# Six transposes of a hybrid decoder layer moved from TensorE to VectorE, and the convolution's step rate set from 0.6 to 0.5

## The chip, the cores and the metric

The kernel runs on one core of one Trainium2 chip. The metric is the device time of one execution in microseconds (us), the median of several runs. The engines named below are TensorE (PE in the profile, PEld its weight loads), VectorE (DVE), ScalarE (ACT), GpSimd (POOL) and SyncE (SP, which issues the DMAs).

## The reference, cut to what matters

One layer, 256 tokens, model width 2048, float32. One projection gives the inputs of three branches, and each branch has its own output projection:

```python
h = rmsnorm(x, g_mix[l])
proj = h @ w_in[l]
u_glu, q_da, k_da, v_da, q_xa, gate_pre = jnp.split(proj, split_idx, axis=-1)

# conformer branch: GLU, causal depthwise convolution of 31 taps, layer norm over channels, swish
a, b = jnp.split(u_glu, 2, axis=-1)
u = a * jax.nn.sigmoid(b)
u = lax.conv_general_dilated(u, w_dw..., padding=[(CONV_WIDTH - 1, 0)],
                             feature_group_count=CONV_CH) + b_dw
y_conv = jax.nn.silu(layernorm(u, g_ln, b_ln)) @ w_conv_out[l]

# differential attention: rotary q and k, two softmaxes per head
q = apply_rope(q_da.reshape(bsz, seq, DA_HEADS, 2, DA_HEAD_DIM), cos, sin)
k = apply_rope(k_da.reshape(bsz, seq, DA_HEADS, 2, DA_HEAD_DIM), cos, sin)
y_da = diff_attention(q, k, v, lam, lambda_init, g_subln[l], w_da_out[l])
y_xa = memory_cross_attention(q_xa, mem_n, w_mem_kv[l], w_xa_out[l])

merged = gates[:, :, 0] * y_conv + gates[:, :, 1] * y_da + gates[:, :, 2] * y_xa
x = x + merged @ w_mix_out[l]
x = x + jnp.square(jax.nn.relu(rmsnorm(x, g_mlp[l]) @ w_up[l])) @ w_down[l]
return rmsnorm(x, g_final)
```

## The kernel before

**Weight groups.** All weights are streamed in order, in groups of 512 output columns (`group`). A group accumulates two PSUM tiles (`acc0` and `acc1`, one for each 128 tokens) over its k-tiles of 128 rows. Weights come in *pairs* of two k-tiles: SyncE loads `raw` (128x1024), ScalarE rounds it to `whi` (L325), VectorE computes `wlo`, the rest (L326, called a weight split here). TensorE then does three products per k-tile and token tile (L346 to L348), 12 matmuls per pair. `raw`, `whi` and `wlo` have four buffers each, so VectorE can be at most four pairs ahead of TensorE. A group with 2048 rows has 8 pairs, one with 1024 rows has 4.

**Order of the groups.** Four groups for the GLU, four for the memory's keys and values, two for the cross-attention's q (xq), two for q, two for k, two for v. Then, for each of four column chunks, three gate groups and the branch outputs in the order cross-attention (reads `xaT`), differential attention (reads `daT`), convolution (reads `cvT`). Then the mixing projection and the MLP.

**Side work.** What must happen between the groups is written as generators ("tasks") in lanes. After each pair `side_step` gives every lane's first task a tick. A task does one step for each unit of credit, and its rate is the credit per tick. When a group needs an input, it calls `finish` on the task that makes it, and the task's remaining steps are then written down at once. A scheduler at build time orders the instructions of each engine from priorities and an estimate of times; on the chip each engine's queue runs in that order.

**The work around the change.**
- `evac_rope` (L731 on) rotates q or k on VectorE when a group ends, into `rot`. The task `transpose_plain` (L261) then transposes it: eight 128x128 transposes on TensorE into the PSUM tile `tr`, copied by ScalarE (L269) into `qT` or `kT`. There are four such groups.
- `conv_half` (L509) does the same for half of the convolution's channels (`sig` into `uT`), then 31 steps of four tap instructions on VectorE (L518, L522). Both halves are in the lane `conv`, one behind the other, at the rate `CONV_RATE`. With the four steps of the transposes each half has 35 steps.
- `conv_norm` (L528) follows in that lane with some 31 steps at rate 1: sums over channels (L536), mean by a matmul into `pm` (L538), subtraction (L541), squares on ScalarE (L546), their sum (L550), a matmul into `pvar` (L554), square root on ScalarE (L557), reciprocal and a correction (L559 to L564), multiplication (L567), then for each of eight channel blocks sigmoid and affine on ScalarE (L573, L575), a product (L577) and the two parts of `cvT` (L578, L579). The first convolution output group reads `cvT`.
- `block_transpose2` (L235) exists already: 16 `STREAM_TRANSPOSE` instructions on VectorE, each moving 32x32 blocks of a 32x256 slice, in four steps of four. Each is ordered behind the weight split that was written last. It serves the memory keys (`kxT`), the cross-attention's q (`xqT`) and later inputs.
- `products` (L879 on) evacuates the three branch outputs on VectorE: `mg` from the cross-attention (L886), then `gate` and `mg` for the other two (L888, L892).

Of the kernel before, what the change touches and what calls it, by code (L numbers as in the profile page):

```python
# [10 lines left out]
F32 = mybir.dt.float32  # L11
# [8 lines left out]
P = 128  # L20
D = 2048
S = 256
NT = S // P
# [4 lines left out]
EPS = 1e-6  # L28
G = 512
KB = 2  # L30
CONV_RATE = 0.6
NORM_RATE = 1.0
WARM = 10
WB = 4
# [73 lines left out]
def decoder_layer_kernel(  # L108
# [6 lines left out]
    nc = tc.nc  # L115
# [6 lines left out]
    psum = ctx.enter_context(tc.tile_pool(name="psum", bufs=2, space=PSUM))  # L122
# [5 lines left out]
    def spawn(gen, lane="t", rate=1.0, hold=0):  # L128
        t = Task(gen, rate, hold)
        lanes[lane].append(t)  # L130
        return t
# [11 lines left out]
    def later(ins, first):  # L143

        tc.add_manual_dep(
            ins.ins, first.ins.name,
            mybir.DependencyInfo(mybir.DependencyClass.NoSync, mybir.DependencyReason.DATA),
            reason="issue order",
        )

    def finish(*tasks):
        for t in tasks:
            if t is not None:
                t.finish()
# [16 lines left out]
    def transpose(dst, src):  # L171
        k = src.shape[0]
        nc.tensor.transpose(dst, src, ident[:k, :k])  # L173
# [10 lines left out]
    def vcol(nm, i):  # L184
        return vec[:, col[nm] + i : col[nm] + i + 1]
# [10 lines left out]
    def both(f):  # L196
        seen = []

        def g(t, ps):
            seen.append(ps)  # L200
            if len(seen) == NT:
                f(seen)

        return g

    def by_tok(a):
        return [a[:, t, :] for t in range(NT)]

    chain = []

    def link(hi, lo):
# [6 lines left out]
    def scaled_parts(st, i, dst, kt, n, gname):  # L218

        his = [  # L220
            nc.scalar.activation(  # L221
                dst.hi(kt + c), st[:, i + c : i + c + 1, :], AF.Copy, scale=vcol(gname, kt + c)
            )
            for c in range(n)
        ]
        los = [
            nc.vector.scalar_tensor_tensor(
                dst.lo(kt + c), st[:, i + c : i + c + 1, :], vcol(gname, kt + c),
                dst.hi(kt + c).bitcast(F32), ALU.mult, ALU.subtract,
            )  # L230
            for c in range(n)
        ]
        return his[-1], los[-1]

    def block_transpose2(src, dst):  # L235

        B = 32
        out_v = dst.rearrange("p j (t s) -> p t j s", t=NT)
        in_v = src.rearrange("p t (j c k) -> p t j c k", c=P // B, k=B)
        for q in range(P // B):  # L240
            for c in range(P // B):
                ins = nc.vector.transpose(  # L242
                    out_v[c * B : (c + 1) * B, :, :, q * B : (q + 1) * B], in_v[q * B : (q + 1) * B, :, :, c, :]
                )
                later(ins, lo_mark[0])
            yield

    def to_parts_dve(src, dst, kt0, gname=None):

        st = work.tile([P, G // P, S], F32, tag="chunk", name="st", bufs=4)  # L250
        yield from block_transpose2(src, st)
        for b in range(0, G // P, 2):
            k = kt0 + b
            if gname is None:
                nc.scalar.copy(dst.hi(k, 2), st[:, b : b + 2, :])  # L255
                nc.vector.tensor_tensor(dst.lo(k, 2), st[:, b : b + 2, :], dst.hi(k, 2).bitcast(F32), op=ALU.subtract)
            else:
                scaled_parts(st, b, dst, k, 2, gname)
            yield

    def transpose_plain(src, dst, kt0, nkt):  # L261

        for b in range(0, nkt, 2):
            ps = psum.tile([P, 2, S], F32, tag="tr", name="tr")
            for c in range(2):
                for t in range(NT):
                    transpose(ps[:, c, t * P : (t + 1) * P], src[t][:, (b + c) * P : (b + c + 1) * P])
            yield
            nc.scalar.copy(dst[:, kt0 + b : kt0 + b + 2, :], ps)  # L269
            yield  # L270


# [219 lines left out]
    uT = units.tile([P, 8, S], F32, tag="unit", name="uT")  # L492
# [15 lines left out]

    def conv_half(g):  # L509
        u = sig[g]  # L510
        yield from transpose_plain(by_tok(u), uT, g * 4, 4)
        cbs = range(g * 4, g * 4 + 4)
        for d in range(TAPS):
            for cb in cbs:
                i = (TAPS - 1 - d) * 8 + cb
                w = taps[:, i : i + 1]
                if d == 0:
                    ins = nc.vector.tensor_scalar(  # L518
                        conv[:, cb, :], uT[:, cb, :], w, vcol("b_dw", cb), ALU.mult, ALU.add
                    )  # L520
                else:
                    ins = nc.vector.scalar_tensor_tensor(  # L522
                        conv[:, cb, d:], uT[:, cb, : S - d], w, conv[:, cb, d:], ALU.mult, ALU.add
                    )
                later(ins, mark[0])
            yield
# [55 lines left out]
    def evac_a(g):  # L582
        def f(ps):
            for t in range(NT):
                nc.vector.scalar_tensor_tensor(
                    sig[g][:, t, :], ps[t], rinv["x"][:, t : t + 1], sig[g][:, t, :], ALU.mult, ALU.mult
                )
            conv_tasks.append(spawn(conv_half(g), "conv", CONV_RATE))
        return both(f)
# [139 lines left out]
    qk_tasks = []  # L729

    def evac_rope(dst, g):  # L731
        def f(ps):
            finish(t_tables)
            H2 = DH // 2
            rot = work.tile([P, NT, G], F32, tag="chunk", bufs=4, name="rot")
            for t in range(NT):
                sc = rinv["x"][:, t : t + 1]
                cs = cosT[:, t, :].unsqueeze(1).to_broadcast([P, 8, H2])
                sn = sinT[:, t, :].unsqueeze(1).to_broadcast([P, 8, H2])
                pv8 = ps[t].rearrange("p (a d) -> p a d", d=H2)  # L740
                ac = work.tile([P, 8, H2], F32, tag="t2k", name="ropec", bufs=4)
                as_ = work.tile([P, 8, H2], F32, tag="t2k", name="ropes", bufs=4)
                nc.vector.scalar_tensor_tensor(ac, pv8, sc, cs, ALU.mult, ALU.mult)
                nc.vector.scalar_tensor_tensor(as_, pv8, sc, sn, ALU.mult, ALU.mult)
                c2 = ac.rearrange("p (m h) d -> p m h d", h=2)
                s2 = as_.rearrange("p (m h) d -> p m h d", h=2)
                o2 = rot[:, t, :].rearrange("p (m h d) -> p m h d", h=2, d=H2)
                nc.vector.tensor_tensor(o2[:, :, 0, :], c2[:, :, 0, :], s2[:, :, 1, :], op=ALU.subtract)
                nc.vector.tensor_tensor(o2[:, :, 1, :], c2[:, :, 1, :], s2[:, :, 0, :], op=ALU.add)
            qk_tasks.append(spawn(transpose_plain(by_tok(rot), dst, g * 4, 4)))  # L750
        return both(f)

    def evac_v(g):
# [276 lines left out]
```

## Time and profile before

| what | value |
|---|---|
| median of three runs | 1585.04 us (1584.47 to 1587.35) |
| profiled execution, its own time | 1584.57 us |
| its span, first to last instruction | 1582.0 us |
| PE busy | 1567.4 us, 99% of the span |
| DVE busy | 1130.4 us, 71% |
| ACT busy | 782.9 us, 49% |
| granted TensorE clock, mean | 0.998 of full speed |

A busy time is the sum of an engine's intervals. A step on one engine is best read from the starts of consecutive instructions, since neighbours overlap a little. The difference between the execution's own time and its span is 2.57 us, outside the instructions.

### The profile page before, as it was taken

What the parts mean: (1) busy time and instruction counts of PE and PEld (TensorE: products, weight loads), DVE (VectorE), ACT (ScalarE), POOL (GpSimd) and SP (SyncE); (2) the same over time, 40 slices, a digit from 0 to 9 for tenths busy, and PEclk for the clock granted to TensorE, in tenths of its full rate; (3) what the DMA queues carried; (4) which work ended last, traced back from release to release, by engine and by line L of the source; (5) the groups of instructions that cost most, each with busy time, mean ns of one, the idle gap of its engine ahead of it and who ended that gap; (6) DMA issues with size and microseconds to landing.
All of it is one profiled execution on the core that took longest, in us unless ns stands there. A gap on an engine that the chain in (4) does not pass through costs nothing.

```text
span 1582.0 us, 18995 instructions
## 1 busy us (share of the span) xinstructions
PE 1567.4 (99%) x6956; PEld 1296.6 (82%) x6956; DVE 1130.4 (71%) x1639; ACT 782.9 (49%) x1007; POOL 23.3 (1%) x35
## 2 busy tenths in 40 slices
PE   9999999999999999999999999999999999999997
PEld 7888788888888888888888788888888888888886
DVE  5699998887877456474598798447864687548864
ACT  7655445454784444444444555335534454445543
POOL 1000000010000000000000000000000000000000
PEclk9999999999999999999999999999999999999999
DMA  9776575556556666667766666666666666666663
GB/s 345 238 247 193 154 219 162 154 151 200 152 172 195 198 192 196 192 192 207 260 188 199 186 195 188 197 194 190 195 195 192 187 196 197 192 197 187 194 195 129
DMA packets 158732, 308.93 MB, mean 195 GB/s; under 512 B 9792, under 2 KB 10048, under 8 KB 158512
## 3 DMA queue, kind: packets, MB, share of 16 engines
q1 hardware_dynamic: 157104, 303.60, 63.0%
q0 software_dynamic: 960, 3.57, 0.8%
q8 instruction: 54, 0.88, 0.2%
q10 hardware_dynamic: 576, 0.56, 0.1%
q14 instruction: 38, 0.31, 0.1%
HBM read 305.60 MB, written 2.10 MB: 194 GB/s over the span
## 4 chain that ended last, share of the span: by engine, by line
PE 95%; DVE 3%; issue 1%; ACT 0%; DMA 0%; POOLq 0%; POOL 0%; ACTq 0%; DVEq 0%
PE acc L346 31%; PE acc L347 31%; PE acc L348 31%; DVE wlo L326 1%; DVE kxT L242 1%; DVE conv L522 1%; PE xs L678 0%; PE xo L711 0%; DVE st L242 0%; PE ds L773 0%; PE do L824 0%; PE tr L173 0%; DMA xt<-in_x_t_dram 0%; ACT whi L325 0%; PE xpt L173 0%
## 5 line engine op out<-in xcount | busy, mean ns | idle before, releaser
L326 DVE TENSOR_TENSOR wlo<-raw,whi 128x1024 fp32r<-128x1024 f32 (+1 forms) x561 | 684.4, 1221 | 413.0 <-ACT whi L325 409.0
L325 ACT CAST whi<-raw 128x1024 fp32r<-128x1024 f32 (+1 forms) x561 | 589.8, 1052 | 689.5 <-PE acc L348 641.7
L347 PE MATMUL acc<-wlo,xT_hi 128*128 128x512 f32 x768 | 300.2, 392 | 1.0 <-DVE wlo L326 1.0
L346 PE MATMUL acc<-whi,xT_hi 128*128 128x512 f32 x768 | 298.3, 395 | 2.8 <-ACT whi L325 2.8
L348 PE MATMUL acc<-whi,xT_lo 128*128 128x512 f32 x768 | 298.7, 392 | 0.0
L346 PE MATMUL acc<-whi,x1T_hi 128*128 128x512 f32 x512 | 198.2, 389 | 1.1 <-ACT x1T_hi L221 1.1
L347 PE MATMUL acc<-wlo,x1T_hi 128*128 128x512 f32 x512 | 199.0, 389 | 0.0
L346 PE MATMUL acc<-whi,ff_hi 128*128 128x512 f32 x512 | 198.7, 390 | 0.0
L347 PE MATMUL acc<-wlo,ff_hi 128*128 128x512 f32 x512 | 198.6, 389 | 0.0
L348 PE MATMUL acc<-whi,x1T_lo 128*128 128x512 f32 x512 | 198.4, 389 | 0.0
L348 PE MATMUL acc<-whi,ff_lo 128*128 128x512 f32 x512 | 197.9, 389 | 0.0
L346 PEld LDWEIGHTS acc<-whi,xT_hi 128*128 128x128 f32 x768 | 144.7, 189 | 32.7 <-ACT whi L325 3.0
L347 PEld LDWEIGHTS acc<-wlo,xT_hi 128*128 128x128 f32 x768 | 144.5, 188 | 31.3 <-DVE wlo L326 2.1
L348 PEld LDWEIGHTS acc<-whi,xT_lo 128*128 128x128 f32 x768 | 144.5, 188 | 29.9
L242 DVE STREAM_TRANSPOSE st<-ru 32x256 f32<-32x256 f32 x256 | 111.6, 436 | 4.1
L346 PEld LDWEIGHTS acc<-whi,x1T_hi 128*128 128x128 f32 x512 | 96.1, 188 | 21.5 <-ACT x1T_hi L221 1.6
L346 PEld LDWEIGHTS acc<-whi,ff_hi 128*128 128x128 f32 x512 | 96.1, 188 | 21.1 <-ACT ff_hi L255 1.4
L347 PEld LDWEIGHTS acc<-wlo,x1T_hi 128*128 128x128 f32 x512 | 96.1, 188 | 20.1 <-DVE wlo L326 0.2
L348 PEld LDWEIGHTS acc<-whi,ff_lo 128*128 128x128 f32 x512 | 96.1, 188 | 20.0
L347 PEld LDWEIGHTS acc<-wlo,ff_hi 128*128 128x128 f32 x512 | 96.1, 188 | 19.9
L348 PEld LDWEIGHTS acc<-whi,x1T_lo 128*128 128x128 f32 x512 | 96.1, 188 | 19.9
L522 DVE SCALAR_TENSOR_TENSOR conv<-uT,taps,conv 128x255 f32<-128x255 f32 (+29 forms) x240 | 98.2, 461 | 0.3
(197 smaller groups left out, 1376.0 us busy)
## 6 DMA issues: line engine op xcount, KB each, us to landing
raw<-in_w_in_dram SPq DMA_DIRECT2D x191, 512.0 KB, 4.3
raw<-in_w_up_dram SPq DMA_DIRECT2D x128, 512.0 KB, 3.8
raw<-in_w_down_dram SPq DMA_DIRECT2D x128, 512.0 KB, 4.7
raw<-in_w_mem_kv_dram SPq DMA_DIRECT2D x32, 512.0 KB, 4.6
raw<-in_w_mix_out_dram SPq DMA_DIRECT2D x32, 512.0 KB, 4.7
raw<-in_w_xa_out_dram SPq DMA_DIRECT2D x16, 512.0 KB, 4.8
raw<-in_w_da_out_dram SPq DMA_DIRECT2D x16, 512.0 KB, 4.7
raw<-in_w_conv_out_dram SPq DMA_DIRECT2D x16, 512.0 KB, 4.7
```

Source lines behind the costliest of these rows:

```text
L242: ins = nc.vector.transpose(out_v[c * B : (c + 1) * B, :, :, q * B : (q + 1) * B], in_v[q * B : (q + 1) * B, :, :, c, :])
L325: hi = nc.scalar.copy(whi[:, cs, :], raw[:, cs, :])
L326: lo_mark[0] = nc.vector.tensor_tensor(wlo[:, cs, :], raw[:, cs, :], whi[:, cs, :].bitcast(F32), op=ALU.subtract)
L346: nc.tensor.matmul(ps[t], hi[:, tt], whi[:, c, :], start=kt == 0, stop=False)
L347: nc.tensor.matmul(ps[t], hi[:, tt], wlo[:, c, :], start=False, stop=False)
L348: return nc.tensor.matmul(ps[t], lo[:, tt], whi[:, c, :], start=False, stop=kt == nkt - 1)
L522: ins = nc.vector.scalar_tensor_tensor(conv[:, cb, d:], uT[:, cb, : S - d], w, conv[:, cb, d:], ALU.mult, ALU.add)
```

## The change

`transpose_plain` and its helper are removed. The six places that used it, q and k (two groups each) and the convolution's input (two halves), call `block_transpose2`. `CONV_RATE` goes from 0.6 to 0.5, one convolution step for every two pairs. Line numbers of the later code fall by 14.

```diff
-CONV_RATE = 0.6
+CONV_RATE = 0.5
...
-    def by_tok(a):
-        return [a[:, t, :] for t in range(NT)]
...
-    def transpose_plain(src, dst, kt0, nkt):
-
-        for b in range(0, nkt, 2):
-            ps = psum.tile([P, 2, S], F32, tag="tr", name="tr")
-            for c in range(2):
-                for t in range(NT):
-                    transpose(ps[:, c, t * P : (t + 1) * P], src[t][:, (b + c) * P : (b + c + 1) * P])
-            yield
-            nc.scalar.copy(dst[:, kt0 + b : kt0 + b + 2, :], ps)
-            yield
...
     def conv_half(g):
         u = sig[g]
-        yield from transpose_plain(by_tok(u), uT, g * 4, 4)
+        yield from block_transpose2(u, uT[:, g * 4 : g * 4 + 4, :])
...
-            qk_tasks.append(spawn(transpose_plain(by_tok(rot), dst, g * 4, 4)))
+            qk_tasks.append(spawn(block_transpose2(rot, dst[:, g * 4 : g * 4 + 4, :])))
```

**The first place is VectorE behind the evacuation of the first q group.** Before, the queue holds rotation, taps and weight splits:

```order
215 L744 SCALAR_TENSOR_TENSOR ropes<-acc_2008,rinv_x,sinT 128x512
216 L714 TENSOR_TENSOR xaT_lo_2217<-xo,xaT_hi_2215 128x512
217 L748 TENSOR_TENSOR rot<-ropec,ropes 128x4x64
218 L749 TENSOR_TENSOR rot<-ropec,ropes 128x4x64
219 L522 SCALAR_TENSOR_TENSOR conv<-uT,taps,conv 128x253 x4
220 L326 TENSOR_TENSOR wlo<-raw,whi 128x1024
221 L684 TENSOR_REDUCE xnm<-xs 128x2
```

After, at the same place:

```order
216 L239 STREAM_TRANSPOSE uT<-sig 32x2x4x32 x4
217 L734 TENSOR_TENSOR rot<-ropec,ropes 128x4x64
218 L735 TENSOR_TENSOR rot<-ropec,ropes 128x4x64
219 L700 TENSOR_TENSOR xaT_lo_2197<-xo,xaT_hi_2195 128x512
220 L670 TENSOR_REDUCE xnm<-xs 128x2
221 L239 STREAM_TRANSPOSE qT<-rot 32x2x4x32 x13
222 L671 TENSOR_SCALAR xnm<-xnm 128x2
223 L239 STREAM_TRANSPOSE qT<-rot 32x2x4x32
224 L312 TENSOR_TENSOR wlo<-raw,whi 128x1024
```

The transposes of q, and those of the convolution's second half, now stand here between two weight splits, 13 and 1 of q's in one stretch; the second half's taps come later.

**The second place is VectorE around the evacuation of the first cross-attention output** (`mg<-acc`). Before, the last rows of the convolution's normalisation stand ahead of it:

```order
408 L577 TENSOR_TENSOR y<-y,sg 128x256
409 L326 TENSOR_TENSOR wlo<-raw,whi 128x1024
410 L577 TENSOR_TENSOR y<-y,sg 128x256
411 L579 TENSOR_TENSOR cvT_lo_4033<-y,cvT_hi_4031 128x256
412 L326 TENSOR_TENSOR wlo<-raw,whi 128x1024
413 L579 TENSOR_TENSOR cvT_lo_4033<-y,cvT_hi_4031 128x256
414 L886 TENSOR_TENSOR mg<-acc_4010,gate 128x512
415 L886 TENSOR_TENSOR mg<-acc_4011,gate 128x512
416 L326 TENSOR_TENSOR wlo<-raw,whi 128x1024 x4
417 L888 TENSOR_TENSOR gate<-acc_4102,gate 128x512
```

After, the last taps and the whole normalisation stand behind it:

```order
403 L872 TENSOR_TENSOR mg<-acc_3965,gate 128x512
404 L872 TENSOR_TENSOR mg<-acc_3966,gate 128x512
405 L508 SCALAR_TENSOR_TENSOR conv<-uT,taps,conv 128x226 x3
406 L312 TENSOR_TENSOR wlo<-raw,whi 128x1024
407 L508 SCALAR_TENSOR_TENSOR conv<-uT,taps,conv 128x226
408 L522 TENSOR_REDUCE lnt<-conv 128x128
409 L312 TENSOR_TENSOR wlo<-raw,whi 128x1024
410 L522 TENSOR_REDUCE lnt<-conv 128x128
411 L312 TENSOR_TENSOR wlo<-raw,whi 128x1024 x2
412 L874 TENSOR_TENSOR gate<-acc_4049,gate 128x512
413 L874 TENSOR_TENSOR gate<-acc_4050,gate 128x512
414 L878 TENSOR_TENSOR mg<-mg,gate 128x512
```

```order
415 L527 TENSOR_TENSOR conv<-conv,pm 128x256 x8
416 L878 TENSOR_TENSOR mg<-mg,gate 128x512
417 L312 TENSOR_TENSOR wlo<-raw,whi 128x1024
418 L536 TENSOR_TENSOR lnt<-sq 128x256
419 L536 TENSOR_TENSOR lnt<-lnt,sq 128x256 x6
420 L542 TENSOR_SCALAR lnt<-pvar 128x256
421 L545 RECIPROCAL lnt<-lnt 128x256
```

The first `cvT_lo` follows seven rows further. The next weight split is 13 rows further, behind six of the eight channel blocks.

**The third place is TensorE at the end of the first differential attention output** (`daT`). Before, the convolution's group follows at once:

```order
1967 L346 MATMUL acc_4103<-whi,daT_hi_3499 128x512
1968 L347 MATMUL acc_4103<-wlo,daT_hi_3499 128x512
1969 L348 MATMUL acc_4103<-whi,daT_lo_3502 128x512
1970 L346 MATMUL acc_4194<-whi,cvT_hi_4031 128x512
1971 L347 MATMUL acc_4194<-wlo,cvT_hi_4031 128x512
```

After, the two small matmuls of the normalisation stand between them:

```order
1952 L333 MATMUL acc_4050<-wlo,daT_hi_3475 128x512
1953 L334 MATMUL acc_4050<-whi,daT_lo_3478 128x512
1954 L524 MATMUL pm<-lnt,ones 128x256
1955 L540 MATMUL pvar<-lnt,ones 128x256
1956 L332 MATMUL acc_4131<-whi,cvT_hi_4197 128x512
1957 L333 MATMUL acc_4131<-wlo,cvT_hi_4197 128x512
```

Before, `pm` and `pvar` stand some 260 and 170 rows ahead of that group, among the gate groups' matmuls. After, no other weight product stands between `daT`'s last one and `cvT`'s first.

## Rows read from the trace of the kernel before

**Rows 1.** Page, part 1: busy time, share of the span and instructions of each engine.

```profile
PE 1567.4 (99%) x6956; PEld 1296.6 (82%) x6956; DVE 1130.4 (71%) x1639; ACT 782.9 (49%) x1007; POOL 23.3 (1%) x35
```

**Rows 2.** Busy time by stretch: start:end length, busy of each engine, clock, DMA.

```profile
160.00:200.00 40.00, 39.01 (x175) 31.64 (x174) 38.11 (x72) 18.11 (x20) 0.00 (x0) 1.00 0.52 154
...
0.00:482.40 482.40, 477.55 (x2156) 396.00 (x2157) 396.34 (x699) 276.13 (x422) 17.04 (x27) 1.00 0.65 199
```

**Rows 3.** The tile tr: instructions, count, duration in ns (min/median/max), first and last start.

```profile
L173 PE MATMUL tr<-ident,rot x32: 270/272/275, 262.4 to 346.7; 128*128 128x128 f32 x32
...
L173 PE MATMUL tr<-ident,sig x16: 270/272/273, 58.3 to 180.2; 128*128 128x128 f32 x16
```

**Rows 4.** The chain that ended last, in order of time: start, us, what.

```profile
58.42 0.44 PE tr L173 x4
```

**Rows 5.** VectorE in time, 177 to 290 us: start, us, instruction [idle before].

```profile
177.43 2.36 DVE L326 TENSOR_TENSOR wlo<-raw,whi 128x1024 fp32r<-128x1024 f32 x2
...
183.14 1.78 DVE L242 STREAM_TRANSPOSE kxT<-kx 32x256 f32<-32x256 f32 x4
184.96 1.58 DVE L522 SCALAR_TENSOR_TENSOR conv<-uT,taps,conv 128x233 f32<-128x233 f32 x4
186.46 1.22 DVE L326 TENSOR_TENSOR wlo<-raw,whi 128x1024 fp32r<-128x1024 f32 x1
...
232.83 7.18 DVE L242 STREAM_TRANSPOSE xqT<-xq 32x256 f32<-32x256 f32 x16
240.04 1.23 DVE L326 TENSOR_TENSOR wlo<-raw,whi 128x1024 fp32r<-128x1024 f32 x1
...
282.38 0.75 DVE L743 SCALAR_TENSOR_TENSOR ropec<-acc,rinv_x,cosT 128x512 f32<-128x512 f32 x1 [0.52 <-PE acc L348]
...
287.50 1.63 DVE L522 SCALAR_TENSOR_TENSOR conv<-uT,taps,conv 128x248 f32<-128x248 f32 x4
```

**Rows 6.** TensorE in time: the first product of daT and of cvT.

```profile
471.70 0.39 PE L346 MATMUL acc<-whi,daT_hi 128*128 128x512 f32 x1
...
482.58 0.39 PE L346 MATMUL acc<-whi,cvT_hi 128*128 128x512 f32 x1
```

**Rows 7.** VectorE in time, 405 to 473 us: the convolution's normalisation.

```profile
405.37 3.91 DVE L536 TENSOR_REDUCE lnt<-conv 128x128 f32<-128x1024 f32 x2
...
419.17 2.73 DVE L541 TENSOR_TENSOR conv<-conv,pm 128x256 f32<-128x256 f32 x8
...
424.42 0.94 DVE L550 TENSOR_TENSOR lnt<-lnt,sq 128x256 f32<-128x256 f32 x2
...
445.52 1.75 DVE L559 RECIPROCAL lnt<-lnt 128x256 f32<-128x256 f32 x1 [1.24 <-ACT lnt L557]
...
450.02 1.77 DVE L567 TENSOR_TENSOR conv<-conv,lnt 128x256 f32<-128x256 f32 x5
...
472.01 0.42 DVE L579 TENSOR_TENSOR cvT_lo<-y,cvT_hi 128x256 fp32r<-128x256 f32 x1
472.35 1.28 DVE L886 TENSOR_TENSOR mg<-acc,gate 128x512 f32<-128x512 f32 x2
```

**Rows 8.** ScalarE in time, 443 to 457 us: the same normalisation.

```profile
443.77 1.28 ACT L557 ACT_TABLE_LOAD   x1
445.06 0.42 ACT L557 ACTIVATE lnt<-lnt 128x256 f32<-128x256 f32 x1
...
452.13 0.60 ACT L573 ACTIVATE sg<-conv,vec 128x256 f32<-128x256 f32 x1
452.64 0.59 ACT L575 ACTIVATE y<-conv,vec 128x256 f32<-128x256 f32 x1
...
455.78 0.40 ACT L578 CAST cvT_hi<-y 128x256 fp32r<-128x256 f32 x1
```

**Rows 9.** Groups of instructions: the table load at the start, its idle time and releaser.

```profile
L221 ACT ACT_TABLE_LOAD x1 | 1.3, 1283 | 5.4 <-DMA xt<-in_x_t_dram 5.4
```

**Rows 10.** Busy time by stretch, the first products after the start.

```profile
8.00:10.60 2.60, 2.60 (x7) 1.98 (x7) 1.61 (x4) 2.03 (x4) 0.00 (x0) 0.50 1.05 404
```

## The prediction

> **What bounds the kernel now.** I read the page's busy times first: PE is busy in 99% of the span [rows 1]. Then the busy times by stretch: up to 482.4 us, where the first convolution output begins, TensorE idles 4.85 us in all, and 0.99 us of this in the one stretch where VectorE was busy for 38.1 of 40 us [rows 2]. The rest lies at the start. So the kernel is a stream of matmuls on TensorE. An edit can gain only what it takes out of that stream, and it loses whatever makes the stream stop. After 482 us nothing changes but the step at its edge, so the sum is made over what lies before it.
>
> **What the change removes.** 32 transposes of q and k and 16 of the convolution's input [rows 3] leave TensorE. Four take 0.44 us of its chain [rows 4], so 48 x 0.11 = 5.3 us, all on the path. Their twelve copies leave ScalarE. These cost nothing, since ScalarE is busy 276 of 482 us [rows 2].
>
> **What it adds.** 6 x 16 = 96 block transposes on VectorE, four in 1.82 us, from 183.14 to 184.96 [rows 5], so 43.7 us. VectorE has 86 us of idle time before 482 us [rows 2], but not everywhere. The 16 of the first convolution half fall where it has room. The other 80 fall in the groups of q, k and v, as the order shows.
>
> I add up VectorE's queue over the 40 weight splits from the second q group to the second v group (five groups): 40 splits at 1.14 to 1.18 (two take 2.36) [rows 5] are 46 us; 80 block transposes 36 us; 60 taps at 0.38 to 0.41 (four take 1.50) are 23.5 us; four rotations at 4.0 us (282.38 to 287.50, less one split) are 16 us; the attention's small steps, by estimate, 7.5 us. The sum is 129 us. TensorE needs 40 pairs of 12 matmuls; four pairs take 482.58 - 471.70 = 10.88 us [rows 6], so 40 pairs take 108.8 us, and the attention's matmuls by estimate 16.5 us at the same rate per column, together 125.3 us. VectorE is thus 3.6 us over, having been at 110 us for the same groups before. Its lead of four buffers, up to 8 us, may cover that. The trace shows a run of 16 transposes between two splits, from 232.83 to 240.04 [rows 5], in a stretch without idle TensorE, and an overload of about the same size that cost 0.99 us [rows 2]. But now runs of 13 and 14 follow each other every 25 us, while the lead is small. I take 3.5 us lost, between 0 and 8.
>
> The Trainium skill (VectorE: DVE Perf Modes, "The three transpose paths" and "Rules for kernel authors") gives 311 ns for 128x128 on VectorE in bf16, and advises TensorE for a full 128x128 transpose. Here eight such tiles take 16 x 0.45 us, 0.9 us each, in float32, so the price is three times the page's. By the page's price the 96 would be an estimated 15 us, and the overload of VectorE would not exist.
>
> The lower rate takes some taps out of the groups of the memory's keys, where VectorE was the limit, at 160 to 200 us [rows 2]. Half of the 0.99 us goes: 0.5 us gained, between 0 and 1.
>
> **What it moves.** This is the largest term. Each half has 35 steps in one lane. At 0.6 the 70 steps take 117 ticks, at 0.5 they take 140. The first half is spawned at tick 16, the convolution output begins at tick 160. Before, the halves end at tick 133, which leaves 27 ticks for 31 steps of normalisation. After, they end at tick 156, which leaves four. The rest is written down in one piece when the output group asks for `cvT`. The order shows it: VectorE's last four taps, both reductions and all behind them stand after the evacuation of the cross-attention output, and TensorE has only `pm` and `pvar` between the last product of `daT` and the first of `cvT`. Before, the last `cvT_lo` was done at 472.4 us, 10 us ahead of its use [rows 6, 7].
>
> The evacuation cannot start before TensorE ends the cross-attention group, and VectorE's queue is in order, so I count from that moment, called 0. TensorE ends `daT` at 10.9 [rows 6].
> - Two evacuations 1.3, taps 1.5, two splits 2.3, two reductions 3.9 [rows 7]: at 9.0 the sums are ready. This is hidden behind `daT`; `pm` runs at 10.9 to 11.5.
> - Two splits that wait for buffers until about 11.6, then the next evacuation with one addition 1.9, eight subtractions 2.7, one more addition and split 1.8: 18.0.
> - Seven additions at 0.45 are 3.1 [rows 7], `pvar` and its use 1.1: 22.2.
> - Table load 1.28 and square root 0.42 [rows 8], reciprocal 1.75, four small steps at 0.45: 27.4. A table load waits for its activation's input, as the first one did for a DMA [rows 9], so it is not hidden.
> - First multiplication 0.3 (five take 1.77) [rows 7], table load 1.28, two sigmoids and two affines at 0.51 [rows 8], a product and the first `cvT_hi` 0.8: 31.8.
>
> So TensorE stands from 11.5 to about 31.5. Then ScalarE makes a block every 1.3 us (two at 0.51, one cast at 0.3), about TensorE's own 1.36 us per k-tile, but three weight casts of 1.06 us stand between the last blocks. This costs some 1 us. The clock also falls: in the first products after the start, behind a pause, it was 0.50, the 1.2 GHz level, for 2.6 us [rows 10], which lost half of that, 1.3 us. Part of it hides behind ScalarE. I take 1 us.
>
> The stall is thus 20 + 1 + 1 = 22 us. Low end 17: the hand count's waits overlap better, or the taps and sums come early. High end 28: half clock for all 48 products of the group adds 9.6 us, of which a third hides.
>
> The Trainium skill (ScalarE: Activation LUTs, "What ACT_TABLE_LOAD costs") adds a drain of 1380 ns to each load. The trace shows the activation 0.01 us behind the load's end, and the load took 1.28 us [rows 8]. By the page two loads would add an estimated 2.8 us, and the stall would be 25 us. I go by the row.
>
> **The sum** against the profiled execution's 1584.57 us (1582.0 us of span and 2.57 us outside; 0.5 us below the median of the runs): -5.3 - 0.5 + 3.5 + 22 = +19.7 us, so 1604.3 us.
>
> **The rivals.**
> - *The normalisation stays covered.* One mechanism would do it: TensorE has enough other products between `daT` and `cvT`, or VectorE stands at least 20 us further ahead, so that the first `cvT_hi` is written before `daT` ends. Then only the small terms stay: 1584.57 - 5.3 - 0.5 + 3.5 = 1582.3 us, or 1578.8 us with no overload. For it: the same chain was hidden before [rows 7]. Against it: the evacuation waits for a group that ends only 10.9 us ahead, and the queue is in order. It decides at a chain of 10.9 us, and mine is 31 us.
> - *VectorE becomes the bound in q, k and v.* The runs of 13 and 14 transposes (6 us each) delay the splits and the attention's small steps by the whole lead each time, 8 to 10 us in all: with the stall some 1610 us. For it: 129 us of work in 125 us. Against it: the run of 16 that cost nothing [rows 5].
> - *The stop is longer.* Half clock for the whole convolution group, or hops between engines that my hand count leaves out (some 25 of them), make 28 us: 1610 us.
>
> **How the numbers follow.** Forecast 1604.3 us: 0.67, with a range of its own from 1598 to 1609. VectorE the bound: 0.14. A longer stop: 0.12. Covered: 0.07, and it falls about half on each side of the bound for "faster". A measurement of this kernel can tell about 0.2%, 3.2 us, from no change. So faster 0.03, same 0.04, slower 0.93. The range goes from 1595, both low ends, to 1615, the high stop with a few us more in q, k and v.
>
> **What would show it.** In the profile after: TensorE idle for some 20 us in one piece near 480 us, released by ScalarE's `cvT_hi` (step right); VectorE then without a weight split from the eight subtractions to the sixth block; the granted clock at the 1.2 GHz level when `cvT` begins; no `tr` among TensorE's groups; VectorE at 95% or more between 250 and 370 us, with TensorE idle for 0 to 8 us there. I am wrong if `cvT` begins without a gap, if the gap is below 15 us, or if TensorE's idle time lies mainly in the q, k and v groups.

## The result, and the profile after

| | median of the runs, us | lowest to highest | span of the profiled run, us |
|---|---|---|---|
| before | 1585.49 (4 runs) | 1584.47 to 1587.35 | 1582.0 |
| after | 1606.86 (4 runs) | 1604.89 to 1607.3 | 1605.3 |

The ratio after to before is 1.0128, with a 95% interval from 1.0115 to 1.014: the changed kernel is 21.4 us slower. The forecast was 1604.3 us.

First the page, as for before in [rows 1]: its busy times by engine, then TensorE and its clock in 40 slices of 40 us.

```profile
PE 1567.8 (98%) x6908; PEld 1292.1 (80%) x6908; DVE 1172.5 (73%) x1735; ACT 778.6 (49%) x995; POOL 24.1 (1%) x35
...
PE   8999999999995999999999999999999999999997
...
PEclk9999999999997999999999999999999999999999
```

Before, every slice of TensorE but the last was a 9. Now the first reads 8, from a start that came 1 us worse in this run, and the slice from 482 to 522 us reads 5, with a 7 for its clock. The busy time of VectorE rose by 42 us [rows 1], about what 96 transposes cost. The others read as before, so the loss has a place. The waits of TensorE name it (releaser, total us, times, longest):

```profile
PE pvar L540 <- DVE lnt L536: 9.6, 1, 9.6
PE acc L332 <- ACT cvT_hi L564: 8.7, 1, 8.7
PE acc L333 <- DVE wlo L312: 4.7, 5, 1.3
```

Two waits of 18.3 us together, each once, belong to the convolution's normalisation. The third group is five waits for weight splits, in the stages where VectorE is overloaded. Busy time by stretch (columns: from and to, length, then busy us of PE, PEld, DVE, ACT, POOL with counts, granted clock, DMA share, GB/s):

```profile
160.00:200.00 40.00, 39.08 (x172) 31.71 (x171) 38.11 (x69) 16.83 (x18) 0.00 (x0) 1.00 0.53 161
200.00:400.00 200.00, 196.12 (x878) 161.51 (x877) 193.71 (x355) 92.07 (x129) 5.24 (x4) 1.00 0.57 175
...
482.00:494.00 12.00, 2.43 (x11) 1.72 (x10) 10.73 (x22) 5.34 (x11) 0.00 (x0) 0.74 0.47 148
494.00:510.00 16.00, 7.34 (x21) 5.31 (x22) 11.33 (x26) 10.46 (x23) 0.00 (x0) 0.56 0.01 2
510.00:520.00 10.00, 10.00 (x46) 8.28 (x45) 5.65 (x9) 5.32 (x9) 0.00 (x0) 1.00 0.52 154
```

The row of before for the q, k and v groups, beside [rows 2]:

```profile
200.00:400.00 200.00, 200.00 (x917) 166.34 (x916) 170.91 (x302) 98.10 (x148) 6.00 (x6) 1.00 0.59 175
```

From 200 to 400 us there are now 3.9 us of idle TensorE where there was none, with VectorE busy for 193.7 of 200 us instead of 170.9. From 482 to 510 us TensorE works for 9.8 of 28 us, and the clock is at 0.56 in the second part. Even the DMA queues stand still there (2 GB/s), since no weight buffer comes free.

The stop itself, TensorE in order of time:

```profile
483.39 0.40 PE L334 MATMUL acc<-whi,daT_lo 128*128 128x512 f32 x1
483.62 0.59 PE L524 MATMUL pm<-lnt,ones 128*128 128x256 f32 x2
493.79 1.22 PE L540 MATMUL pvar<-lnt,ones 128*128 128x256 f32 x2 [9.57 <-DVE lnt L536]
503.66 0.79 PE L332 MATMUL acc<-whi,cvT_hi 128*128 128x512 f32 x1 [8.65 <-ACT cvT_hi L564]
504.25 0.63 PE L333 MATMUL acc<-wlo,cvT_hi 128*128 128x512 f32 x1
...
508.60 0.39 PE L332 MATMUL acc<-whi,cvT_hi 128*128 128x512 f32 x1
```

From the end of `daT` at 483.62 to the first `cvT` product 20.0 us pass; 1.8 of them pass while `pm` and `pvar` run, which before ran at 418.4 and 441.8 us, far ahead of this place [rows 6]. Then the products follow each other every 0.43 us, the 1.2 GHz level, until 508.60, and every 0.23 us from there.

VectorE over the same time, beside [rows 7]:

```profile
472.45 1.28 DVE L872 TENSOR_TENSOR mg<-acc,gate 128x512 f32<-128x512 f32 x2
...
479.41 1.99 DVE L522 TENSOR_REDUCE lnt<-conv 128x128 f32<-128x1024 f32 x1
481.32 2.35 DVE L312 TENSOR_TENSOR wlo<-raw,whi 128x1024 fp32r<-128x1024 f32 x2
483.58 1.28 DVE L874 TENSOR_TENSOR gate<-acc,gate 128x512 f32<-128x512 f32 x2
...
485.38 2.73 DVE L527 TENSOR_TENSOR conv<-conv,pm 128x256 f32<-128x256 f32 x8
...
488.63 1.22 DVE L312 TENSOR_TENSOR wlo<-raw,whi 128x1024 fp32r<-128x1024 f32 x1
...
495.95 1.75 DVE L545 RECIPROCAL lnt<-lnt 128x256 f32<-128x256 f32 x1 [0.48 <-ACT lnt L543]
...
499.44 2.77 DVE L553 TENSOR_TENSOR conv<-conv,lnt 128x256 f32<-128x256 f32 x8
...
511.04 1.22 DVE L312 TENSOR_TENSOR wlo<-raw,whi 128x1024 fp32r<-128x1024 f32 x1 [0.51 <-ACT whi L311]
```

The same reductions, subtractions, reciprocal and multiplications that stood ahead of 472 us before now stand behind the evacuation at 472.45. They are a serial chain: `pm` waits for both reductions, the subtractions for `pm`, `pvar` for the last addition, and so on. No weight split runs from 489.8 to 511.0.

### The profile page after: what moved, and what is told of

The parts are those of the page before. It is cut to its first block, busy times and chain, and to the rows that moved or that the text cites. A ratio compares the mean times of both kernels' runs of the same rounds, so it can differ in the third digit from the quotient of the medians.

```text
span 1605.3 us, 18989 instructions
## 1 busy us (share of the span) xinstructions
PE 1567.8 (98%) x6908; PEld 1292.1 (80%) x6908; DVE 1172.5 (73%) x1735; ACT 778.6 (49%) x995; POOL 24.1 (1%) x35
## 4 chain that ended last, share of the span: by engine, by line
PE 86%; DVE 10%; issue 2%; DMA 1%; ACT 1%; SPq 0%; DVEq 0%; POOLq 0%; POOL 0%; ACTq 0%
PE acc L332 28%; PE acc L333 28%; PE acc L334 28%; DVE wlo L312 3%; DVE conv L508 1%; DMA raw<-in_w_in_dram 1%; DVE qT L239 1%; DVE kT L239 1%; DVE st L239 0%; DVE xqT L239 0%; DVE uT L239 0%; DVE ropes L730 0%; ACT whi L311 0%; PE do L810 0%; DVE ropec L729 0%
## 5 line engine op out<-in xcount | busy, mean ns | idle before, releaser
L332 PE MATMUL acc<-whi,xT_hi 128*128 128x512 f32 x768 | 289.5, 391 | 3.7 <-ACT whi L311 2.5
L332 PEld LDWEIGHTS acc<-whi,x1T_hi 128*128 128x128 f32 x512 | 96.1, 188 | 21.5 <-ACT x1T_hi L218 1.6
```

Source lines behind the costliest of these rows:

```text
L332: nc.tensor.matmul(ps[t], hi[:, tt], whi[:, c, :], start=kt == 0, stop=False)
```

## The experiments

Two changes are mixed in the kernel: where 48 transposes are done, and how fast the taps are written down (0.5 instead of 0.6). My theory put +21.5 us on the rate (+22 for the stop, -0.5 in the key groups) and -1.8 us on the transposes (-5.3 removed, +3.5 for an overloaded VectorE). The rival was that the transposes on VectorE make the loss. The kernel before, run beside each of these, took 1585.3 to 1585.9 us, and the ratios are to that.

| kernel | median, us | ratio to before | 95% interval |
|---|---|---|---|
| before, rate 0.5 (pe_rate05) | 1607.39 | 1.0136 | 1.0122 to 1.015 |
| after, rate 0.6 (blocks_rate06) | 1586.06 | 1.0002 | 0.9993 to 1.0011 |
| before, q and k alone moved to VectorE (qk_blocks) | 1585.22 | 0.9997 | 0.9988 to 1.0006 |
| before, convolution's input alone moved (conv_blocks) | 1584.85 | 0.999 | 0.9981 to 0.9999 |
| before, the 48 transposes left out (no_transposes) | 1579.65 | 0.9962 | 0.9949 to 0.9976 |
| after, rate 0.55 (blocks_rate055) | 1597.2 | 1.0072 | 1.0058 to 1.0086 |
| after, rate 0.8 (blocks_rate08) | 1591.65 | 1.0038 | 1.0024 to 1.0053 |
| after, TensorE kept busy in the stop (warm_stop) | 1604.56 | 1.012 | 1.0107 to 1.0134 |
| after, without the refinement (no_refine) | 1604.56 | 1.012 | 1.0104 to 1.0135 |
| taps by stage (blocks_spread) | 1584.18 | 0.9991 | 0.9982 to 0.9999 |
| taps by stage, transposes spread, 0.40 (smooth_040) | 1583.89 | 0.999 | 0.9981 to 0.9999 |
| taps by stage, transposes spread, 0.35 (smooth_035) | 1582.15 | 0.9975 | 0.9966 to 0.9984 |

**The rate alone.** The kernel before with

```
-CONV_RATE = 0.6
+CONV_RATE = 0.5
```

> The kernel before with the rate 0.5 alone; q, k and the convolution's input are still transposed on TensorE. Theory (the rate makes the stop): TensorE idles 17 to 20 us in two pieces between daT and cvT as in the changed kernel, the clock falls to the 1.2 GHz level behind it, and no overload stands before it: 1585.5 + 22 = 1607 us (1603 to 1611), the same as the changed kernel within 4 us. Rival (the transposes on VectorE are the loss): no stop, 1585 us (1583 to 1588).

1607.39 us, as slow as the changed kernel. TensorE in order of time:

```profile
484.12 0.59 PE L538 MATMUL pm<-lnt,ones 128*128 128x256 f32 x2
493.90 1.22 PE L554 MATMUL pvar<-lnt,ones 128*128 128x256 f32 x2 [9.18 <-DVE lnt L550]
503.78 0.79 PE L346 MATMUL acc<-whi,cvT_hi 128*128 128x512 f32 x1 [8.66 <-ACT cvT_hi L578]
```

The same two waits, 17.8 us, with every transpose still on TensorE. The rate alone costs 21.5 us (1607.39 - 1585.93).

**The transposes alone.** The changed kernel with

```
-CONV_RATE = 0.5
+CONV_RATE = 0.6
```

> The changed kernel with the convolution's rate put back to 0.6, so that all 96 block transposes stay on VectorE and only the moved taps are undone. Theory (the lower rate makes the stop, the transposes cost a few us): the stop of 18 us near 483 us is gone, since the last taps stand two weight splits behind those of the kernel before and the normalisation has some 10 us to spare there; what is left is -5.3 us for the transposes that TensorE no longer does and some 4 us of idle TensorE in the q, k and v groups, so 1584 us (1581 to 1588). Rival (the transposes on VectorE are the loss, they hold back the normalisation and the splits): TensorE still stops for over 10 us near 480 us, or idles over 10 us between 200 and 400 us, and the time stays above 1597 us.

1586.06 us, inside the expected 1581 to 1588: the stop is gone, so 20.8 us of the changed kernel's time were the rate. But the 5.3 us of the transposes were given back in full. Two rows, the q, k and v groups and the place of the former stop:

```profile
200.00:400.00 200.00, 196.72 (x873) 160.88 (x872) 197.75 (x369) 91.13 (x126) 4.54 (x4) 1.00 0.59 174
...
482.00:520.00 38.00, 38.00 (x169) 31.48 (x168) 29.66 (x41) 16.75 (x18) 0.00 (x0) 1.00 0.69 204
```

VectorE is busy for 197.75 of 200 us, and TensorE is no longer its own bound there.

**The removed term alone.** In the kernel before

```
 for b in range(0, nkt, 2):
-    ps = psum.tile([P, 2, S], F32, tag="tr", name="tr")
-    for c in range(2):
-        for t in range(NT):
-            transpose(ps[...], src[t][...])
     yield
-    nc.scalar.copy(dst[...], ps)
     yield
 ...
+nc.gpsimd.memset(uT, 0.01)
 ...
+nc.gpsimd.memset(qT, 0.01)
+nc.gpsimd.memset(kT, 0.01)
```

> The kernel before with the 48 transposes of q, k and the convolution's input and their twelve copies left out, and nothing in their place: uT, qT and kT are filled once with a constant on GpSimd, so the convolution and the differential attention work on constants. Taps, rate and all else as before. This is the removed term alone. Theory (the transposes stand in TensorE's stream, 0.11 us each, all on the path): 1585.5 - 5.3 = 1580.2 us (1579 to 1581.5). Rival (part of them ran in gaps that TensorE had anyway, or their weight loads were hidden): 1582.5 to 1585 us.

1579.65 us, 6.1 us less than before (interval 3.8 to 8.1): the 5.3 us hold. Some 0.4 us of the 6.1 lie outside the instructions: an execution's own time was 2.3 to 2.6 us longer than its span in the runs of before, 2.1 us here, and 1.9 to 2.0 us in every run with some of the six transposes moved to VectorE; why was not tried. In the profiled runs I measure the stretch from the first `sig` to the first `cvT_hi` product, so that the start, which differs by up to 2.6 us from one profiled run to another, falls out. Rows by tile: duration min, median, max, then first and last start. Before, then without the transposes:

```profile
L504 ACT ACTIVATE sig<-acc,rinv_x x4: 679/688/689, 38.1 to 76.9; 128x512 f32<-128x512 f32 x4
L346 PE MATMUL acc<-whi,cvT_hi x64: 388/389/390, 482.6 to 786.5; 128*128 128x512 f32 x64
```

```profile
L500 ACT ACTIVATE sig<-acc,rinv_x x4: 680/688/689, 38.4 to 76.3; 128x512 f32<-128x512 f32 x4
L341 PE MATMUL acc<-whi,cvT_hi x64: 388/390/390, 477.9 to 781.9; 128*128 128x512 f32 x64
```

482.6 - 38.1 = 444.5 us before and 477.9 - 38.4 = 439.5 us without: 5.0 us. At rate 0.6 with all transposes on VectorE:

```profile
L490 ACT ACTIVATE sig<-acc,rinv_x x4: 682/688/690, 40.0 to 78.3; 128x512 f32<-128x512 f32 x4
L332 PE MATMUL acc<-whi,cvT_hi x64: 389/389/389, 485.8 to 789.8; 128*128 128x512 f32 x64
```

485.8 - 40.0 = 445.8 us, so the 96 block transposes cost 6.3 us there. The idle time of PE shows only 3.3 us of it between 200 and 400 us; at 160 to 200 it is 1.59 us, and 1.55 in the kernel without the transposes. Reading the idle column alone would miss the rest: a matmul's record is 0.39 us long while the next one starts 0.23 us after it, so a wait of under 0.16 us leaves no gap, and a longer one shows 0.16 us too short. The weight loads (PEld) don't overlap each other, 0.19 us every 0.23, and their busy time comes nearer. Without the transposes:

```profile
200.00:400.00 200.00, 200.00 (x905) 166.53 (x904) 172.47 (x307) 97.20 (x143) 4.09 (x6) 1.00 0.60 177
```

166.53 us against 160.88 with them is 3.4% less, by estimate 6.8 us of 200.

**The two halves of the move.** The kernel before with one replacement each:

```
-qk_tasks.append(spawn(transpose_plain(by_tok(rot), dst, g * 4, 4)))
+qk_tasks.append(spawn(block_transpose2(rot, dst[:, g * 4 : g * 4 + 4, :])))
```

> The kernel before with q and k alone transposed on VectorE (64 block transposes), the convolution's input on TensorE, rate 0.6. Theory: 32 x 0.11 = 3.5 us leave TensorE's stream, and VectorE's overload in the q, k and v groups gives about as much back: 1585 us (1582 to 1588), with 2 to 5 us of idle TensorE between 240 and 400 us and no stop near 480 us. Rival (the transposes on VectorE are the loss): over 1592 us, with idle TensorE of 8 us or more in those groups.

```
-yield from transpose_plain(by_tok(u), uT, g * 4, 4)
+yield from block_transpose2(u, uT[:, g * 4 : g * 4 + 4, :])
```

> The kernel before with the convolution's input alone transposed on VectorE (32 block transposes), q and k on TensorE, rate 0.6. Theory: 16 x 0.11 = 1.8 us leave TensorE's stream; the first half's 16 lie where VectorE has room, the second half's 16 fall near 200 us, beside no transposes of q and k, and cost 0 to 1 us: 1584 us (1583 to 1585.5). Rival (block transposes delay the splits wherever they stand): 1587 us or more.

1585.22 and 1584.85 us, both inside what the theory expected. q and k give their 3.5 us back, with 2.2 us of visible idle time from 200 to 400 us. The convolution's input keeps about 1 us by the medians, at the edge of what can be told from no change. Half of that lies outside the instructions, and its stretch from the first `sig` to the first `cvT_hi` product is as long as before (444.4 against 444.5 us), so a gain in the work itself isn't shown.

**How the stop is made up.** The changed kernel at 0.55, where a part of the normalisation stands ahead of `daT`'s evacuation:

```
-CONV_RATE = 0.5
+CONV_RATE = 0.55
```

> The changed kernel at rate 0.55. In this order of instructions both reductions, the eight subtractions, the additions of squares and the addition of EPS to pvar stand ahead of or between splits before daT's evacuation; from the second of the four small steps on the normalisation stands in one piece with it. Theory (the stop is the part of the normalisation's chain that stands behind daT's end, added up step by step): evacuation with its addition 1.9 us, a split 1.15, three small steps 1.5, first multiplication 0.3, table load 1.28, sigmoid and affine 1.0, product and cast 0.7, so a stop of 7 to 9 us in one piece, released by cvT_hi: 1586 + 8 = 1594 us (1590 to 1598). Rival (the stop is all or nothing, it comes whole as soon as the normalisation isn't done when the output group asks for cvT): a stop of 15 us or more, 1604 to 1608 us.

```profile
492.90 0.79 PE L332 MATMUL acc<-whi,cvT_hi 128*128 128x512 f32 x1 [8.31 <-ACT cvT_hi L564]
...
498.19 0.42 PE L332 MATMUL acc<-whi,cvT_hi 128*128 128x512 f32 x1
```

One wait of 8.31 us, as added up from the order: the stop isn't all or nothing. The time, 1597.2 us, is 3 us above the 1594 that I expected, since I left out the clock: the products behind the stop run at the 1.2 GHz level here too, for 5.3 us, until 498.19. The next run prices that in the longer stop.

```
 nc.tensor.matmul(pm, ones, nwt, ...)
+pw2 = psum.tile([P, P], F32, tag="at", name="pw1")
+for _ in range(42):
+    nc.tensor.matmul(pw2, ones, ones, start=True, stop=True)
 ...
 nc.vector.tensor_scalar(var, pvar, EPS, None, ALU.add)
+pw2 = psum.tile([P, P], F32, tag="at", name="pw2")
+for _ in range(34):
+    nc.tensor.matmul(pw2, ones, var[:, 0:P], start=True, stop=True)
```

> The changed kernel with 42 idle 128x128 matmuls of a constant beside pm and 34 behind pvar, so that TensorE works through most of the stop; their results go nowhere. Theory (of the stop's price some 1 us is the clock, which fell to the 1.2 GHz level): the granted clock stays at the 2.4 GHz level when cvT begins, its first 20 products follow each other every 0.23 us instead of 0.43, and since ScalarE gives a block only every 1.3 us, 0.8 to 2.2 us come back: 1605.5 us (1604 to 1606.5). Rival (ScalarE's blocks limit the group at either clock): no gain, 1606.9 us, with TensorE waiting for cvT_hi several times instead.

```profile
484.93 8.87 PE L527 MATMUL pw<-ones 128*128 128x128 f32 x78
493.95 0.70 PE L543 MATMUL pvar<-lnt,ones 128*128 128x256 f32 x2 [0.16 <-DVE lnt L539]
495.17 7.86 PE L548 MATMUL pw<-lnt,ones 128*128 128x128 f32 x68 [0.52 <-DVE lnt L545]
503.31 0.50 PE L332 MATMUL acc<-whi,cvT_hi 128*128 128x512 f32 x1 [0.28 <-ACT cvT_hi L570]
503.65 0.39 PE L333 MATMUL acc<-wlo,cvT_hi 128*128 128x512 f32 x1
```

`cvT` begins at almost the same time (503.31 instead of 503.66), but its products follow each other at full clock from the first one. 1604.56 against 1606.86 us: 2.3 us come back, and the profiled stretch from the first `sig` to the end is as much shorter (1562.4 against 1564.7 us). So the clock costs 2.3 us of the 21.5, just above the 0.8 to 2.2 that I expected, and ScalarE's blocks don't limit the group: its only wait for `cvT_hi` is the first one.

```
 nc.vector.reciprocal(rstd, std)
 yield
-nc.vector.tensor_tensor(nwt, rstd, rstd, op=ALU.mult)
-nc.vector.tensor_tensor(nwt, nwt, var, op=ALU.mult)
-nc.vector.tensor_scalar(nwt, nwt, -0.5, 1.5, ALU.mult, ALU.add)
-nc.vector.tensor_tensor(rstd, rstd, nwt, op=ALU.mult)
```

> The changed kernel with the four small steps behind the reciprocal (the refinement of the square root) left out. Theory (the stop is a serial chain on VectorE and ScalarE, every step on it counts in full): the second piece of the stop is shorter by 1.74 us, the time from the reciprocal's end to the first multiplication in the changed kernel: 1605.1 us (1604 to 1606), 6.9 us instead of 8.65 before cvT. Rival (the stop is set by something beside the chain, such as weight buffers or the second table load): the second piece stays at 8 us or more and the time within 0.5 us of 1606.9.

```profile
500.31 0.80 PE L332 MATMUL acc<-whi,cvT_hi 128*128 128x512 f32 x1 [6.95 <-ACT cvT_hi L560]
```

The second wait fell from 8.65 to 6.95 us, by 1.70 where 1.74 was expected. The median fell by 2.3 us, but from the first `sig` to the end the profiled run is only 1.0 us shorter (1563.7 against 1564.7 us); the start makes up the rest there. So these four small steps count in full in the wait, and nothing beside the chain sets it.

**The other side of the rate.**

```
-CONV_RATE = 0.5
+CONV_RATE = 0.8
```

> The changed kernel at rate 0.8. The taps of the first half then fall into the groups of the convolution's input and of the memory's keys at 24 to 28 per eight splits instead of 16 at 0.5, where VectorE is busy for 35 to 38 of 40 us already. Theory (VectorE has room for the taps only in some stages; too high a rate overloads the early ones as too low a one uncovers the normalisation): no stop near 480 us, but idle TensorE of 5 to 12 us between 120 and 280 us: 1592 us (1586 to 1600). Rival (only the end of the taps matters): 1581 to 1585 us.

1591.65 us, where 1592 was expected. The stretch at 120 to 160 us and its neighbour:

```profile
120.00:160.00 40.00, 40.00 (x178) 33.12 (x177) 40.00 (x93) 17.34 (x19) 0.00 (x0) 1.00 0.64 200
160.00:200.00 40.00, 37.59 (x164) 30.14 (x163) 39.03 (x75) 18.01 (x21) 0.00 (x0) 1.00 0.54 160
```

VectorE has no idle time left at 120 to 160 us, and TensorE waits behind it. The overload doesn't stay in the early groups as I had expected: TensorE is idle for 4.8 us between 120 and 280 us and for 4.0 more up to 400. There was no stop near 480 us. So too high a rate costs time as too low a one does.

**A version that beats both.** Where does the gain of 5.3 us survive? In the q, k and v groups VectorE must have less to do, and room for it is at 400 to 480 us. So the taps got a rate by stage, and in two further kernels q and k's four transposing steps a place at every second tick.

```
-CONV_RATE = 0.5
-NORM_RATE = 1.0
+CONV_RATE = 0.65      (smooth_035, smooth_040: 0.6)
+NORM_RATE = 2.0
+for t in conv_tasks:              # ahead of q
+    t.rate = 0.35     (smooth_040: 0.4)
+for t in conv_tasks:              # behind v
+    t.rate = 2.0      (smooth_040: 1.5)
 # smooth_035 and smooth_040 alone:
-qk_tasks.append(spawn(block_transpose2(rot, ...)))
+qk_tasks.append(spawn(block_transpose2(rot, ...), "t", 0.5))
```

> All 96 block transposes on VectorE, but the taps' rate goes by stage: 0.65 until q begins, 0.35 in the groups of q, k and v, 2.0 behind them, and 2.0 for the normalisation. In this order the q, k and v groups hold 8 to 12 taps each instead of 15 to 23 at rate 0.6, and the normalisation ends on the same split as in the kernel before. Theory (at rate 0.6 the gain of 5.3 us was given back because VectorE had more to do in those groups than TensorE): 40 taps x 0.39 = 15 us leave the groups, their idle time falls below 1.5 us, no stop comes near 480 us, 1581.5 us (1579.5 to 1584). Rival (runs of 13 to 16 block transposes between two splits stall TensorE whatever the taps do): idle time of 4 us or more in those groups, 1584.5 to 1588 us.

> All 96 block transposes on VectorE; taps at 0.6 until q begins, 0.35 in q, k and v, 2.0 behind them, normalisation 2.0; and each of the q and k tiles' four transposing steps at every second tick instead of every tick. With the taps spread but the transposes in runs, VectorE had 8.5 to 10.5 us of other work between two splits at four places in the q, k and v groups (265.39 to 273.69 us is one), longer than its lead of up to 8 us. Here the longest such stretch in those groups is 5 to 6.5 us by the order and the durations of the trace. Theory (what stalls TensorE is a stretch between two splits that is longer than the lead): idle time between 200 and 400 us falls from 3.1 us to below 1 us, TensorE keeps most of the 5.3 us: 1581.5 us (1580 to 1583.5). Rival (the block transposes' volume is the cost, wherever they stand): idle time of 3 us or more there, 1584 us or more. The normalisation's last block is written four splits later than in the kernel before, so a third outcome is a wait for cvT_lo behind 483 us, of up to 3 us.

> As the run with 0.35, but taps at 0.4 in q, k and v and 1.5 behind them; the normalisation's last block is then written two splits later than in the kernel before, as at rate 0.6, and the longest stretch without a split in the q, k and v groups is 7.2 us. Theory (a stretch between two splits longer than the lead): one short stall of up to 1 us in the k groups, none near 480 us, 1582 us (1580.5 to 1584). Rival (volume of block transposes): 1584 us or more.

The first kernel came out at 1584.18 us, just outside the 1579.5 to 1584 that I expected: VectorE was as busy (193.65 of 200 us) and TensorE idle for 3.1 us, between the theory's 1.5 and the rival's 4. 0.7 of this came at 332.57 us. The larger part stood in the first q group, right behind a run of 15 block transposes of `xq`, from 236.43 to 243.15 us:

```profile
244.46 0.50 PE L333 MATMUL acc<-wlo,xT_hi 128*128 128x512 f32 x1 [1.34 <-DVE wlo L312]
248.49 0.50 PE L333 MATMUL acc<-wlo,xT_hi 128*128 128x512 f32 x1 [1.02 <-DVE wlo L312]
```

The stretch from 265.39 to 273.69 us that I had named as a cause in the next expectation left TensorE busy throughout. VectorE's lead tells the two apart, counted from the starts of the products (12 per pair): it was 2.2 pairs when the last split ahead of the run ended at 236.51 us (before had 3.0 at this run), and 3.8 pairs at 264.80 us, ahead of the longer stretch. So a stretch without a split hurts only where it outlasts the lead. That the rate of 0.65 had used up the lead ahead of `xq` is likely, but no run parts it.

The kernel with 0.6, 0.35 and transposes at every second tick came out at 1582.15 us, 3.7 us below before, and beats both kernels:

```profile
200.00:400.00 200.00, 199.17 (x895) 164.99 (x894) 194.56 (x359) 96.24 (x141) 3.29 (x6) 1.00 0.59 176
```

VectorE does as much in this stretch as in the changed kernel (194.56 against 193.71 us), and TensorE is idle for 0.8 us instead of 3.9. The number of block transposes is thus not what costs; when they and the taps are written down is. Load and place both changed, though: from the first split of the second q group to the first behind the v groups VectorE works 120.7 us here and 126.9 in the changed kernel, since the convolution's second half is transposed earlier. The gain must come from the transposes taken off TensorE: the kernel before with taps by stage alone wasn't run, but its TensorE had no idle time from 200 to 482 us that the taps could have given back. The wait for `cvT_lo` that I had held possible did not come. Two edits part this run from the one before it, the rate of 0.65 and the tick of the transposes; which of them gave how much wasn't run. With 0.4, instead of one short stall in the k groups, there were three in the v groups (346.09, 359.38 and 364.14 us), of 2.7 us together, and the time was 1583.89 us, at the upper end.

## Why the prediction was right, point by point

It named the direction, the place and the mechanism, and the size within 2.6 us. About 0.9 of these are its base (1584.57 us, the profiled execution, where the median of the runs became 1585.49). The rest comes from the two terms of the transposes. Inside the stop a clock 1.3 us dearer and weight casts 1 us cheaper than forecast cancel, by luck.

- **-5.3 us for the transposes taken off TensorE: right.** The runs show -6.1 us by the medians, 0.4 of them outside the instructions, and -5.0 in the profiled stretch.
- **+3.5 us for an overloaded VectorE (0 to 8): right in kind, too small.** At rate 0.6 the block transposes cost 6.4 us (1586.06 - 1579.65); at 0.5 some 5.6 us, by 1606.86 less 1607.39 - 6.1. The sum of 129 us of work was 2 us too high: from 250.94 to 381.32 us, the same 40 splits, VectorE worked 126.9 us, and 129 less the 125.3 that TensorE needs is 3.7, not 3.6. So the overload was smaller than counted and the loss larger. What failed is the reason given for the size: an overload summed over five groups does not tell what single stretches without a split cost. "The run of 16 that cost nothing" [rows 5] lasted 7.1 us and began with a lead of 3.0 pairs (84 pairs split, 972 products started at 232.91 us), of which 0.6 was left when the next split ended. In the changed kernel the lead at 295.22 us is again 3.0 pairs (103 pairs split, 1200 products started), but taps, rotations, the attention's small steps and 13 transposes make the stretch 9.2 us long. TensorE needs 8.2 us for three pairs (10.88 us for four [rows 6]) and waits at the end of it:

```profile
294.00 1.22 DVE L312 TENSOR_TENSOR wlo<-raw,whi 128x1024 fp32r<-128x1024 f32 x1
...
298.59 5.82 DVE L239 STREAM_TRANSPOSE qT<-rot 32x256 f32<-32x256 f32 x13
304.44 1.23 DVE L312 TENSOR_TENSOR wlo<-raw,whi 128x1024 fp32r<-128x1024 f32 x1
...
```

```profile
305.72 0.50 PE L333 MATMUL acc<-wlo,xT_hi 128*128 128x512 f32 x1 [1.18 <-DVE wlo L312]
```

- **-0.5 us in the key groups: wrong, and small.** The idle time from 160 to 200 us went from 0.99 to 0.92 us, and to 0.91 with the rate alone.
- **+22 us for the uncovered normalisation: right.** The rate alone costs 21.5 us. Counted from the evacuation at 472.45 us, the sums were ready at 9.0 us (forecast 9.0), `pvar` was used by 23.0 (22.2), the four small steps were done at 27.0 (27.4), and the first `cvT` product came at 31.2 (31.8). So "TensorE stands from 11.5 to about 31.5" holds to half a microsecond. It does so in two pieces of 9.6 and 8.7 us with `pvar` between them, and not in one piece of some 20 us as the sign said, although the list of steps had `pvar` at its place. Each piece is under the 15 us named as a sign of being wrong; the whole, 18.2 us without `pm` and `pvar`, is not. Of its two additions, ScalarE's weight casts cost nothing (forecast 1) and the clock 2.3 us (forecast 1): I had let a part of it hide behind ScalarE.
- **"A table load waits for its activation's input": wrong once, right once.** ScalarE in order of time:

```profile
491.71 1.28 ACT L543 ACT_TABLE_LOAD   x1
495.50 0.42 ACT L543 ACTIVATE lnt<-lnt 128x256 f32<-128x256 f32 x1 [2.51 <-DVE lnt L542]
499.95 1.28 ACT L559 ACT_TABLE_LOAD   x1 [4.03 <-DVE conv L553]
501.24 0.60 ACT L559 ACTIVATE sg<-conv,vec 128x256 f32<-128x256 f32 x1
```

  The load for the square root began 3.3 us ahead of its input, which VectorE wrote from 495.05 us, and was hidden. The load for the sigmoid waited for the first multiplication and stood on the chain. The 1.28 us that the first saved make up for the 0.8 us by which the chain was late up to `pvar`. Behind the second load the activation began 0.01 us after its end, as in [rows 8], so the drain of 1380 ns that the Trainium skill (ScalarE: Activation LUTs, "What ACT_TABLE_LOAD costs") adds does not show here either.
- **The price of a block transpose: right.** 16 in 7.16 us (5.82 for 13), 0.9 us for a 128x128 tile in float32, three times the 311 ns that the Trainium skill gives for bf16 (VectorE: DVE Perf Modes, "The three transpose paths"). Its advice ("Rules for kernel authors") to use TensorE for a 128x128 transpose agrees with the kernels at rate 0.6, which gained little or nothing from the move, and not with the one whose taps and transposes are both spread, which gained 3.7 us.
- **The rivals.** The normalisation stayed uncovered. VectorE as the bound cost 6 us, not the 8 to 10 on top of the stop that the rival asked for. The longer stop did not come. "VectorE without a weight split from the eight subtractions to the sixth block" had one exception, the split at 488.63 us.

## What to carry to other kernels

A step that only changes how early off-path work is written down can uncover a chain that was hidden: count the steps of the chain, the time that each takes, and the last piece of the bound engine's work that can cover it, before lowering a rate. Work moved from the bound engine to a busy one gains only if no stretch without a piece of work for the bound engine outlasts the busy one's lead; the same 96 transposes gave 0 us at one rate of the taps, and 3.7 us once taps, normalisation and transposes were written down at other times. Where an engine's records overlap, its idle time reads too low; a stream whose records do not overlap, here the weight loads, comes nearer.

## What the runs showed of the hardware that I had not expected

- Behind the stop of 8.3 us at rate 0.55 the products ran at the 1.2 GHz level for 5.3 us, longer than the 4.9 us behind the stop of 18.2 us at 0.5. With TensorE busy on idle matmuls through an 18 us stop the granted clock stayed at 1.00, and 2.3 us came back.
- The time of an execution outside its span was 2.3 to 2.6 us in the runs of before and 1.9 to 2.0 us in those with some of the six transposes moved to VectorE.
- Of two table loads in one chain, one began 3.3 us ahead of its activation's input and one waited for it. Why they differ wasn't tried.
